# Differential attention: the split of the transposed probabilities moves to ACT and VectorE, the difference of the maps to GpSimd, the scores into one five-bank PSUM tile

## The chip, the cores and the metric

The kernel runs on one core of a Trainium2 chip. The metric is the device time of one execution in microseconds (us). Before the change it was 3203.99 us, the median of three runs (3201.15 to 3204.88).

## The reference, cut to what matters

The program computes one step of a two-layer backbone on 1024 latent tokens and 128 context tokens, all in fp32: in layer 0 differential attention, in layer 1 windowed attention, after each a SwiGLU feed-forward part, with norms and modulation around them. The change touches only the differential attention of the latent tokens: 8 heads, 1024 queries, 1280 keys (256 cached and 1024 own). Each head has two maps of scores with 64 columns each:

```python
s = jnp.einsum('bqhmd,bkhmd->bhmqk', qi, k).astype(jnp.float32) * scale
p = jax.nn.softmax(s, axis=-1)
a = p[:, :, 0] - lam * p[:, :, 1]
return jnp.einsum('bhqk,bkhe->bqhe', a.astype(v.dtype), v)
```

## The kernel before, in words

Matrix products keep fp32 accuracy by splitting an operand into a rounded half (hi) and a remainder (lo), both of type fp32r, and adding three products.

`diff_attention` works on 32 pairs: each of the 8 heads has four pairs of 128-row query blocks. In a pair, i is the block (0 or 1) and m the map (0 or 1). The steps are methods of `Pair`, one letter each:

- S: six matmuls write the 128x1280 scores of (m, i) into PSUM (line 737). The tile has three banks of 512 columns, and there are two such tiles, taken in turn.
- R: VectorE's maximum over the 1280 scores (line 744). E: ACT's exponential of them into SBUF, with the row sum (line 749).
- c: two small VectorE instructions for the factor of map 1 (lines 755 and 756). C: VectorE adds both maps, `a = e1 * factor + e0` (line 761).
- T: TensorE transposes `a`, four 128x128 blocks (two in the last group, g = 2) into one PSUM bank (line 768).
- V: ACT copies the transposed group to SBUF as `a32` (line 773). P: GpSimd rounds it to hi (line 110, the helper `pool_round`) and subtracts for lo (line 784); in the very last pair VectorE does the subtraction.
- A: three matmuls of one key block with the values (lines 793 to 795), ten A per pair. X, B, Y: copy, transpose back, copy out and store.

The order is written out by hand: `ROUND` is a list of tokens, and a token such as T112 means step T, group (or map) 1, block 1, of the pair two rounds back. So E011 and R111 are work on the second block of the pair before, S000 on the first of the present one. Each engine executes its own instructions strictly in the order of this list; engines run beside one another and wait only for what an instruction needs. One pass of the list is a round, there are 32, and `DRAIN` finishes the last pairs. The W token splits a piece of the output weights in every second round (lines 102 and 103).

PSUM has eight banks. Before, the scores take six, the transposes (tag `t`) one, the accumulator `av` one. The exponentials `e` have four SBUF buffers, `a` two.

Two other places are named by the prediction. `turn_hT` (lines 164 and 165) splits a transposed PSUM tile with ACT and VectorE. `Halves.first` (lines 1395 and 1396) lets ACT and VectorE both copy the same transposed PSUM tile; line 1413 is a copy by ACT of the second tile, which for the last, half-wide pair is the same tile as that of line 1396, in columns 64 to 127 instead of 0 to 63 of each block.

Of the kernel before, what the change touches and what calls it, by code (L numbers as in the profile page):

```python
# [9 lines left out]
F32 = mybir.dt.float32  # L10
F32R = mybir.dt.float32r
BF16 = mybir.dt.bfloat16
AF = mybir.ActivationFunctionType
ALU = mybir.AluOpType
AX = mybir.AxisListType
# [3 lines left out]
P = 128  # L19
# [11 lines left out]
DH = 8  # L31
# [13 lines left out]
def hybrid_step(ctx: ExitStack, tc: tile.TileContext, x_prompt, x_sample, cache_diff_k, cache_diff_v,  # L45
# [5 lines left out]
    act, dve, pool, pe = nc.scalar, nc.vector, nc.gpsimd, nc.tensor  # L51
# [57 lines left out]
    def pool_round(out, in_):  # L109
        pool.tensor_scalar(out=out, in0=in_, scalar1=1.0, scalar2=0.0, op0=ALU.mult, op1=ALU.add)  # L110
# [588 lines left out]
    def diff_kv(sb, h):  # L699
        K = sb.tile([P, 2, (NTB + NCB) * P], F32R, name="K")  # L700
        dma(out=K.bitcast(F32), in_=kT_d[0][2 * h:2 * h + 2].rearrange("m p t -> p m t"))
        V = sb.tile([P, NTB + NCB, 2, P], F32R, name="V")
        dma(out=V.bitcast(F32), in_=v_d[0][:, h].rearrange("(t p) f d -> p t f d", p=P))
        return K, V
# [11 lines left out]
    def diff_attention(op, s1_all, wo_pool, pre, kv0, q0):  # L716
        NKB = NCB + 8
        NK = NKB * P
        with sbuf("da") as sb, psum("dap") as ps:
            class Pair:  # L720


                def __init__(self, h, tbs):
                    self.h, self.tbs, self.last = h, tbs, (h, tbs[0]) == (DH - 1, 6)
                    self.S, self.e, self.a, self.s2, self.nm = {}, {}, {}, {}, {}
                    self.tp, self.a32, self.aT, self.kb = {}, {}, {}, 0

                def s1(self, i):
                    return s1_all[:, self.tbs[i], self.h:self.h + 1]

                def step_S(self, m, i):

                    S = self.S[i, m] = ps.tile([P, 3 * 512], F32, name="S", tag="S", bufs=2)
                    for j in range(0, NK, 512):
                        n = min(NK - j, 512)
                        for f in range(2):
                            pe.matmul(S[:, j:j + n], lhsT=self.q[:, f, m, i * P:(i + 1) * P],  # L737
                                      rhs=kv[self.h][0][:, m, j:j + n], start=(f == 0), stop=(f == 1))

                def step_R(self, m, i):  # L740
                    if m == 0:
                        self.nm[i] = sb.tile([P, 2], F32, name="nm", tag="sm", bufs=8)
                        self.s2[i] = sb.tile([P, 2], F32, name="s2", tag="sm", bufs=8)
                    dve.tensor_reduce(out=self.nm[i][:, m:m + 1], in_=self.S[i, m][:, 0:NK], axis=AX.X, op=ALU.max,  # L744
                                      negate=True)

                def step_E(self, m, i):
                    e = self.e[i, m] = sb.tile([P, NK], F32, name="e", tag="e", bufs=4)
                    act.activation(out=e, in_=self.S[i, m][:, 0:NK], func=AF.Exp, bias=self.nm[i][:, m:m + 1],  # L749
                                   accum_out=self.s1(i) if m == 0 else self.s2[i][:, 0:1])  # L750

                def step_c(self, _, i):
# [5 lines left out]
                def step_C(self, _, i):  # L758

                    self.a[i] = sb.tile([P, NK], F32, name="a", tag="a", bufs=2)  # L760
                    dve.scalar_tensor_tensor(out=self.a[i], in0=self.e[i, 1], scalar=self.s2[i][:, 1:2], in1=self.e[i, 0],
                                             op0=ALU.mult, op1=ALU.add)

                def step_T(self, g, i):

                    tp = self.tp[i, g] = ps.tile([P, 4, P], F32, name="tpa", tag="t", bufs=1)
                    for t in range(4 * g, min(4 * g + 4, NKB)):
                        pe.transpose(tp[:, t - 4 * g, :], self.a[i][:, t * P:(t + 1) * P], ident)

                def step_V(self, g, i):  # L770
                    n = min(4, NKB - 4 * g)
                    x = self.a32[i, g] = sb.tile([P, 4, P], F32, name="a32", tag="a32", bufs=2)
                    act.copy(out=x[:, 0:n, :], in_=self.tp[i, g][:, 0:n, :])  # L773

                def step_P(self, g, i):

                    n = min(4, NKB - 4 * g)
                    if g not in self.aT:
                        self.aT[g] = sb.tile([P, 2, 4 if g < 2 else 2, 2 * P], F32R, name="aT",
                                             tag="aT" if g < 2 else "aTb", bufs=4 if g < 2 else 2)  # L780
                    hi, lo = [self.aT[g][:, f, 0:n, i * P:(i + 1) * P] for f in range(2)]
                    x = self.a32[i, g][:, 0:n, :]
                    pool_round(hi, x)
                    (dve if self.last else pool).tensor_tensor(out=lo, in0=x, in1=hi.bitcast(F32), op=ALU.subtract)  # L784

                def step_A(self, _, __):

# [13 lines left out]

                def step_B(self, _, __):

                    self.ot = ps.tile([P, 4, P], F32, name="tpo", tag="t", bufs=1)
                    for i in range(2):
                        pe.transpose(self.ot[:, i, :], self.oT[:, i * P:(i + 1) * P], ident)

                def step_Y(self, _, __):
# [2 lines left out]
                    t0 = self.tbs[0] * P  # L811
                    dma(out=o_d[t0:t0 + 2 * P, self.h * P:(self.h + 1) * P].rearrange("(t p) d -> p t d", p=P), in_=ot)

            pairs = [Pair(h, (tb, tb + 1)) for h in range(DH) for tb in range(0, 8, 2)]
            kv = {0: kv0}
            pairs[0].q = q0
# [2 lines left out]
            def wo_piece(i):  # L819
# [5 lines left out]

            ROUND = ("c001 A003 T012 A003 V202 V102 S000 R111 P213 T112 P002 A003 A003 E011 A003 P202 V012 "
                     "C001 P102 E111 T212 R000 V112 W000 S100 P012 R100 T001 X003 A002 V212 c011 E000 A002 "
                     "A002 B003 S010 V001 C011 Y003 T201 R010 A002 P112 E100 A002 T101 S110").split()  # L830


            DRAIN = ("c001 l1 A003 A003 V202 P213 l0 T012 V102 R111 A003 A003 P002 E011 P202 V012 A003 "
# [3 lines left out]
                     "A001 A001 A001 A001 P211 A001 A001 A001 n0 s11 X001 B001 Y001 n1").split()  # L837
            n = len(pairs)

            def run(token, i):  # L840
                j = i - int(token[-1])
                if token[0] in "lsn":
                    op.early({"l": "load", "s": "stat", "n": "scale"}[token[0]], *[int(x) for x in token[1:]])
                elif token[0] == "W":
                    if i % 2 == 0 and i < 32:
                        wo_piece(i // 2)
                elif 0 <= j < n:
                    getattr(pairs[j], "step_" + token[0])(int(token[1]), int(token[2]))

            with tc.manual_schedule(engines=ENGINES):  # L850
                for i in range(n):
                    if i + 1 < n:
                        x = pairs[i + 1]
                        x.q = diff_q((pre, sb)[(i + 1) % 2], x.h, x.tbs)
                    if i % 4 == 2:
                        h = pairs[i].h + 1
                        if h < DH:
                            kv[h] = diff_kv((pre, sb)[h % 2], h)
                    for token in ROUND:
                        run(token, i)  # L860
                for token in DRAIN:
                    run(token, n)
            return wo

    class Prompts:
# [29 lines left out]
        def score(self, h0):  # L895
            q, e = self.q[h0], self.e[h0]
            nm = small8("nm8")
            for half in range(2):
                ms = slice(4 * half, 4 * half + 4)
                S = self.bank("pS")  # L900
                for m in range(4):
                    for f in range(2):
                        pe.matmul(S[:, m, :], lhsT=q[f][:, 4 * half + m, :], rhs=self.K[h0][:, 4 * half + m, :],
                                  start=(f == 0), stop=(f == 1))
# [61 lines left out]
    def swa_kv(sb, g, rooms=None):  # L966
        K = rooms[0] if rooms else sb.tile([P, (NTB + NCB) * P], F32R, name="K")
        dma(out=K.bitcast(F32), in_=kT_d[1][g])
        V = rooms[1] if rooms else sb.tile([P, NTB + NCB, 2, HD], F32R, name="V")
        dma(out=V.bitcast(F32), in_=v_d[1][:, g].rearrange("(t p) f d -> p t f d", p=P))  # L970
        return K, V
# [10 lines left out]
    def swa_attention(op, wo_pool, pre, kv0, q0):  # L982
        with sbuf("sa") as sb, psum("sap") as ps:
# [133 lines left out]
            for g in range(SKV):  # L1117
                for tbs in ((0, 1), (2, 3), (4, 5), (6, 7)):
                    pair = {"tbs": tbs}
                    for half, tb in enumerate(tbs):  # L1120
# [5 lines left out]

            ROUND = ("S00 R00 T42 E31 C42 K11 A02 A12 E00 T01 S10 L32 L42 C01 K21 L01 "
                     "R10 B03 A22 D03 M03 E10 S20 R20 T11 C11 E20 A32 S30 R30 L11 T21 "
# [5 lines left out]
            with tc.manual_schedule(engines=ENGINES):  # L1134
                for i in range(n + LAST):
# [5 lines left out]
                    if u0 and u0.tb == 4 and u0.g + 1 < SKV:  # L1141
                        kv[u0.g + 1] = swa_kv((pre, sb)[(u0.g + 1) % 2], u0.g + 1)
                    for token in ROUND:
                        j = i - int(token[2])
# [768 lines left out]
    f = la.f  # L1913
# [87 lines left out]
```

## Time and profile before

| | |
|---|---|
| median of 3 runs | 3203.99 us |
| the profiled execution's own time | 3199.07 us |
| its span | 3197.3 us |
| TensorE busy | 3001.8 us (94%) |
| VectorE busy | 2048.6 us (64%) |
| ACT busy | 1421.9 us (44%) |
| GpSimd busy | 1361.9 us (43%) |
| mean granted TensorE clock | 0.981 |

The profile comes from one execution. The span runs from the first to the last instruction. PE is TensorE's matmul, PEld its weight load (which overlaps matmuls), DVE is VectorE, ACT is ScalarE, POOL is GpSimd. Busy shares are means over the whole program; the stage of the change is only some 13% of it, so the rows below are mostly of that stage alone. A granted clock of 1.00 is 2.4 GHz, 0.50 is 1.2 GHz.

### The profile page before, as it was taken

The numbers are of one execution on the slowest core, as the hardware profiler recorded it, in microseconds if no ns is written. First come the engines' busy times: TensorE is split into PE (matmuls) and PEld (weight loads), VectorE is DVE, ScalarE is ACT, GpSimd is POOL, SyncE is SP. The second block draws the span as 40 slices with busy tenths as digits, with TensorE's granted clock in tenths as the row PEclk, the third lists the DMA queues.
The fourth block names the chain that finished last, engine by engine and source line by source line (L and its number), as shares of the span: only waits on it lengthen the run. The fifth ranks groups of instructions, "written<-read, shape, count | busy, mean of one in ns | idle before, by whom it ended". The sixth has DMA issues, their size and how long they took to land.

```text
span 3197.3 us, 47914 instructions
## 1 busy us (share of the span) xinstructions
PE 3001.8 (94%) x17998; PEld 2636.8 (82%) x17998; DVE 2048.6 (64%) x2789; ACT 1421.9 (44%) x2764; POOL 1361.9 (43%) x1186
## 2 busy tenths in 40 slices
PE   8999988998896999999999899999987999999999
PEld 5888777777776999999878787777767999998887
DVE  6786388888566777753786643999567633334544
ACT  6332267777554333333444323777433333333442
POOL 2553289999343444442021343666333433340101
PEclk9999999999998999999999999999988999999999
DMA  6675633332422434335765354433432322226564
GB/s 214 200 228 179 201 112 114 116 118 94 130 100 80 129 109 129 109 97 177 252 216 195 130 173 125 116 115 99 142 107 81 108 64 83 66 80 211 185 199 149
DMA packets 373808, 442.23 MB, mean 138 GB/s; under 512 B 26804, under 2 KB 295644, under 8 KB 373576
## 3 DMA queue, kind: packets, MB, share of 16 engines
q1 hardware_dynamic: 373576, 439.16, 43.6%
q8 instruction: 142, 2.33, 0.3%
q14 instruction: 90, 0.74, 0.1%
HBM read 335.71 MB, written 103.37 MB: 137 GB/s over the span
## 4 chain that ended last, share of the span: by engine, by line
PE 67%; POOL 14%; DVE 9%; ACT 4%; issue 3%; DMA 2%; SPq 1%; DVEq 0%; ACTq 0%; POOLq 0%
POOL aT L784 7%; PE guX L1518 6%; PE guX L1519 6%; PE guX L1520 6%; PE dacc L1635 5%; PE dacc L1637 5%; PE dacc L1636 5%; POOL aT L110 4%; PE qacc L556 4%; PE qacc L558 4%; PE qacc L557 4%; PE guY L1518 3%; PE guY L1520 3%; PE guY L1519 3%; PE guZ L1518 1%
## 5 line engine op out<-in xcount | busy, mean ns | idle before, releaser
L1551 POOL TENSOR_TENSOR sg<-sg,U 128x256 f32<-128x256 f32 x88 | 74.9, 851 | 563.4 <-ACT sg L1550 553.1
L1635 PE MATMUL dacc<-fh,ahl 128*128 128x512 f32 x792 | 312.0, 394 | 2.3 <-DVE U L1554 2.3
L1636 PE MATMUL dacc<-fl,ahl 128*128 128x512 f32 x792 | 310.7, 392 | 0.0
L1637 PE MATMUL dacc<-fh,ahl 128*128 128x512 f32 x792 | 310.7, 392 | 0.0
L556 PE MATMUL qacc<-whi,hh 128*128 128x512 f32 x648 | 259.7, 401 | 1.3 <-ACT hh L431 1.3
L558 PE MATMUL qacc<-whi,hl 128*128 128x512 f32 x648 | 254.9, 393 | 0.0
L557 PE MATMUL qacc<-wlo,hh 128*128 128x512 f32 x648 | 254.2, 392 | 0.6 <-DVE wlo L106 0.6
L154 POOL TENSOR_TENSOR xt<-yacc,xt 128x1024 f32<-128x1024 f32 (+1 forms) x19 | 49.7, 2621 | 459.9 <-DVE yacc L153 242.0
L784 POOL TENSOR_TENSOR aT<-a,aT 128x512 fp32r<-128x512 f32 x186 | 237.3, 1276 | 15.5
L1620 DVE TENSOR_TENSOR fl<-fraw,fh 128x1024 fp32r<-128x1024 f32 x132 | 165.4, 1253 | 121.3 <-ACT fh L1619 120.7
L744 DVE TENSOR_REDUCE nm<-S 128x1 f32<-128x1280 f32 x128 | 190.2, 1486 | 51.1 <-PE S L737 51.1
L1619 ACT CAST fh<-fraw 128x1024 fp32r<-128x1024 f32 x132 | 138.4, 1048 | 170.8 <-DMA fraw<-in_w_down_dram 156.7
L737 PE MATMUL S<-K,q 128*128 128x512 f32 (+1 forms) x768 | 184.5, 377 | 12.9 <-ACT e L749 8.9
L266 DVE SCALAR_TENSOR_TENSOR macc<-wmod,sc,macc 128x512 f32<-128x512 f32 x196 | 186.1, 992 | 0.0
L1635 PEld LDWEIGHTS dacc<-fh,ahl 128*128 128x128 f32 x792 | 149.2, 188 | 36.4 <-DVE U L1554 3.1
L1637 PEld LDWEIGHTS dacc<-fh,ahl 128*128 128x128 f32 x792 | 149.0, 188 | 33.7
L1636 PEld LDWEIGHTS dacc<-fl,ahl 128*128 128x128 f32 x792 | 149.1, 188 | 32.9
L749 ACT ACTIVATE e<-S,nm 128x1280 f32<-128x1280 f32 x128 | 171.4, 1339 | 7.2 <-DVE nm L744 7.1
L737 PEld LDWEIGHTS S<-K,q 128*128 128x128 f32 x768 | 137.5, 193 | 43.8 <-ACT e L749 19.0
L578 ACT CAST xT<-tpx 128x512 fp32r<-128x512 f32 x127 | 68.5, 592 | 236.5 <-issue 125.3
L110 POOL TENSOR_SCALAR aT<-a 128x512 fp32r<-128x512 f32 x192 | 154.0, 802 | 22.7 <-ACT a L773 22.7
L1490 DVE TENSOR_TENSOR fl<-fsum,fh 128x1024 fp32r<-128x1024 f32 x84 | 102.3, 1218 | 81.3 <-ACT fh L1488 81.3
(369 smaller groups left out, 9726.7 us busy)
## 6 DMA issues: line engine op xcount, KB each, us to landing
fraw<-in_w_down_dram SPq DMA_DIRECT2D x132, 512.0 KB
wmod<-in_w_mod_dram SPq DMA_DIRECT2D x112, 256.0 KB
araw<-a_d SPq DMA_DIRECT2D x132, 192.0 KB
fraw<-in_w_gate_dram SPq DMA_DIRECT2D x44, 512.0 KB
fraw<-in_w_up_dram SPq DMA_DIRECT2D x42, 512.0 KB
qT_d<-xT SPq DMA_DIRECT2D x36, 512.0 KB
q<-qT_d SPq DMA_DIRECT2D x64, 256.0 KB
wraw<-in_w_qkv_diff_dram SPq DMA_DIRECT2D x24, 512.0 KB
```

The lines of the kernel that those rows point to most:

```text
L110: pool.tensor_scalar(out=out, in0=in_, scalar1=1.0, scalar2=0.0, op0=ALU.mult, op1=ALU.add)
L556: pe.matmul(acc, lhsT=xh, rhs=hi[:, a, :], start=(kb == 0), stop=False)
L557: pe.matmul(acc, lhsT=xh, rhs=lo[:, a, :], start=False, stop=False)
L558: pe.matmul(acc, lhsT=xl, rhs=hi[:, a, :], start=False, stop=(kb == KB - 1))
L737: pe.matmul(S[:, j:j + n], lhsT=self.q[:, f, m, i * P:(i + 1) * P], rhs=kv[self.h][0][:, m, j:j + n], start=(f == 0), stop=(f == 1))
L784: (dve if self.last else pool).tensor_tensor(out=lo, in0=x, in1=hi.bitcast(F32), op=ALU.subtract)
L1518: pe.matmul(o, lhsT=hi[:, kb, :], rhs=xh[:, kb, :], start=(first and kb == 0), stop=False, **more)
L1519: pe.matmul(o, lhsT=hi[:, kb, :], rhs=xl[:, kb, :], start=False, stop=False, **more)
L1520: pe.matmul(o, lhsT=lo[:, kb, :], rhs=xh[:, kb, :], start=False, stop=(kb == 3), **more)
L1635: pe.matmul(acc, lhsT=ah, rhs=hi[:, cs], start=(d == 0), stop=False)
L1636: pe.matmul(acc, lhsT=ah, rhs=lo[:, cs], start=False, stop=False)
L1637: pe.matmul(acc, lhsT=al, rhs=hi[:, cs], start=False, stop=(d == NDF - 1))
```

## The change

The scores become one tile, allocated once, of five banks (2560 columns): map 0 in columns 0 to 1279, map 1 in columns 1280 to 2559, for every block and pair. Each map's matmuls are cut where a bank ends, three pieces and six matmuls as before (1280 to 1535, 1536 to 2047, 2048 to 2559 for map 1). The bank that this frees gives the transposes a second buffer. V now writes hi (`aT`, fp32r) directly from PSUM, P is a VectorE subtraction that reads PSUM, and `a32` is gone. C becomes two GpSimd instructions. The special case of the last pair goes. ROUND and DRAIN get another order.

```diff
-                    S = self.S[i, m] = ps.tile([P, 3 * 512], F32, name="S", tag="S", bufs=2)
-                    for j in range(0, NK, 512):
-                        n = min(NK - j, 512)
+                    j0 = m * NK
+                    S = self.S[i, m] = scores[:, j0:j0 + NK]
+                    cuts = [0] + [c - j0 for c in range(512, 5 * 512, 512) if j0 < c < j0 + NK] + [NK]
+                    for j, j1 in zip(cuts, cuts[1:]):
                         for f in range(2):
-                            pe.matmul(S[:, j:j + n], lhsT=self.q[:, f, m, i * P:(i + 1) * P],
-                                      rhs=kv[self.h][0][:, m, j:j + n], start=(f == 0), stop=(f == 1))
+                            pe.matmul(S[:, j:j1], lhsT=self.q[:, f, m, i * P:(i + 1) * P],
+                                      rhs=kv[self.h][0][:, m, j:j1], start=(f == 0), stop=(f == 1))
...
-                    dve.tensor_reduce(out=self.nm[i][:, m:m + 1], in_=self.S[i, m][:, 0:NK], axis=AX.X, op=ALU.max,
-                                      negate=True)
+                    dve.tensor_reduce(out=self.nm[i][:, m:m + 1], in_=self.S[i, m], axis=AX.X, op=ALU.max, negate=True)
...
-                    act.activation(out=e, in_=self.S[i, m][:, 0:NK], func=AF.Exp, bias=self.nm[i][:, m:m + 1],
+                    act.activation(out=e, in_=self.S[i, m], func=AF.Exp, bias=self.nm[i][:, m:m + 1],
...
-                    dve.scalar_tensor_tensor(out=self.a[i], in0=self.e[i, 1], scalar=self.s2[i][:, 1:2], in1=self.e[i, 0],
-                                             op0=ALU.mult, op1=ALU.add)
+                    pool.tensor_scalar(out=self.a[i], in0=self.e[i, 1], scalar1=self.s2[i][:, 1:2], scalar2=None,
+                                       op0=ALU.mult)
+                    pool.tensor_tensor(out=self.a[i], in0=self.a[i], in1=self.e[i, 0], op=ALU.add)
...
-                    tp = self.tp[i, g] = ps.tile([P, 4, P], F32, name="tpa", tag="t", bufs=1)
+                    tp = self.tp[i, g] = ps.tile([P, 4, P], F32, name="tpa", tag="t", bufs=2)
...
-                    x = self.a32[i, g] = sb.tile([P, 4, P], F32, name="a32", tag="a32", bufs=2)
-                    act.copy(out=x[:, 0:n, :], in_=self.tp[i, g][:, 0:n, :])
...
-                    pool_round(hi, x)
-                    (dve if self.last else pool).tensor_tensor(out=lo, in0=x, in1=hi.bitcast(F32), op=ALU.subtract)
+                def step_V(self, g, i):
+
+                    x, hi, _ = self.halves(g, i)
+                    act.copy(out=hi, in_=x)
+
+                def step_P(self, g, i):
+
+                    x, hi, lo = self.halves(g, i)
+                    dve.tensor_tensor(out=lo, in0=x, in1=hi.bitcast(F32), op=ALU.subtract)
...
+            scores = ps.tile([P, 5 * 512], F32, name="S", tag="S", bufs=1)
...
-            ROUND = ("c001 A003 T012 A003 V202 V102 S000 R111 P213 T112 P002 A003 A003 E011 A003 P202 V012 "
-                     "C001 P102 E111 T212 R000 V112 W000 S100 P012 R100 T001 X003 A002 V212 c011 E000 A002 "
-                     "A002 B003 S010 V001 C011 Y003 T201 R010 A002 P112 E100 A002 T101 S110").split()
+            ROUND = ("c001 A003 T012 A003 V102 E011 S000 R111 P102 T112 A003 V012 A003 P012 C001 A003 T212 "
+                     "V112 E111 R000 P112 W000 S100 T001 V212 R100 P212 X003 A002 c011 E000 A002 A002 B003 "
+                     "V001 S010 C011 P001 Y003 T201 A002 R010 V201 E100 A002 T101 P201 S110").split()
```

The helper `halves` returns the transposed group in PSUM and the two halves of `aT` that it is split into.

## Rows read from the trace of the kernel before

**Rows 1.** Busy time by engine in one stretch of the stage (busy us, instruction count).

```profile
core 0: us, PE busy (x) PEld busy (x) DVE busy (x) ACT busy (x) POOL busy (x), PEclk, DMA share, GB/s
600.00:700.00 100.00, 89.88 (x596) 78.28 (x594) 87.16 (x84) 71.07 (x130) 96.00 (x96) 1.00 0.38 121
```

**Rows 2.** The chain of waits, 370 to 860 us; pieces are start, duration, what.

```profile
by line: POOL aT L784 47.6%; POOL aT L110 29.2%; issue 4.0%; ACT junk L1265 2.0%; PE S L737 1.7%; SPq L888 1.6%; DMA V<-o_d 1.5%; PE qacc L558 1.1%; PE qacc L556 1.1%; PE qacc L557 1.1%; DVE nm L744 0.9%; DMA wraw<-in_w_o_diff_dram 0.9%; SP
...
463.76 1.84 POOL aT L110
...
783.63 1.83 POOL aT L110
```

**Rows 3.** Lines 110 and 784 over the whole trace: ns minimum/median/maximum, forms.

```profile
L110 POOL TENSOR_SCALAR aT<-a x192: 404/617/1873, 406.0 to 811.7; 128x512 fp32r<-128x512 f32 x128, 128x256 fp32r<-128x256 f32 x64
...
L784 POOL TENSOR_TENSOR aT<-a,aT x186: 725/1287/2393, 406.7 to 803.0; 128x512 fp32r<-128x512 f32 x124, 128x256 fp32r<-128x256 f32 x62
```

**Rows 4.** Instruction groups by shape, 450 to 700 us: total busy us, mean ns.

```profile
L744 DVE TENSOR_REDUCE nm<-S 128x1 f32<-128x1280 f32 x79 | 117.4, 1486 | 30.9 <-PE S L737 30.9
...
L761 DVE SCALAR_TENSOR_TENSOR a<-e,s 128x1280 f32<-128x1280 f32 x40 | 79.8, 1996 | 0.7
...
L773 ACT COPY a<-tpa 128x512 f32<-128x512 f32 x79 | 46.4, 587 | 37.1 <-POOL aT L784 32.3 <-PE tpa L768 4.8
...
L756 DVE SCALAR_TENSOR_TENSOR s<-s_all,neglam,s 128x1 f32<-128x1 f32 x39 | 14.2, 363 | 1.4
...
L755 DVE RECIPROCAL s<-s 128x1 f32<-128x1 f32 x39 | 5.9, 152 | 0.0
```

**Rows 5.** Line 165, a VectorE subtraction that reads PSUM, over the trace.

```profile
L165 DVE TENSOR_TENSOR hl<-tp_n,hh x30: 673/680/693, 57.9 to 1831.2; 128x512 fp32r<-128x512 f32 x30
```

**Rows 6.** Instructions in order of time: start, us, what, [idle before, releaser].

```profile
906.24 0.59 ACT L1395 CAST B11h<-tp_n 128x512 fp32r<-128x512 f32 x1 [0.25 <-PE tp_n L1388]
...
906.85 1.29 DVE L1396 COPY raw<-tp_n 128x512 f32<-128x512 f32 x2 [0.47 <-ACT B11h L1395]
...
2420.52 0.74 DVE L1396 COPY raw<-tp_n 128x256 f32<-128x256 f32 x2
...
2421.29 0.37 ACT L1413 COPY raw<-tp_n 128x256 f32<-128x256 f32 x1 [3.65 <-DVE raw L1396]
```

**Rows 7.** In order of time, a round's TensorE work: scores, transposes, values.

```profile
604.65 0.46 PEld L768 LDWEIGHTS tpa<-ident,a 128*128 128x128 f32 x4
604.75 0.60 PE L768 MATMUL tpa<-ident,a 128*128 128x128 f32 x4
...
605.54 0.28 PE L793 MATMUL av<-aT,V 128*128 128x256 f32 x1
...
605.90 0.28 PE L793 MATMUL av<-aT,V 128*128 128x256 f32 x1
...
610.63 1.23 PEld L737 LDWEIGHTS S<-K,q 128*128 128x128 f32 x6
610.66 1.41 PE L737 MATMUL S<-K,q 128*128 128x512 f32 x6
```

**Rows 8.** The chain of waits where the stage starts, one behind the other.

```profile
394.32 2.52 PE S L737 x6
396.86 1.50 DVE nm L744
398.39 1.43 ACT e L749 x2
399.86 4.54 PE S L737 x12
```

**Rows 9.** TensorE's granted clock: two stretches, and an instruction behind an idle time.

```profile
394.32:396.84 2.52, 2.52 (x7) 2.10 (x8) 0.75 (x1) 1.42 (x2) 0.00 (x0) 0.50 0.95 367
...
992.04 1.31 PE L1388 MATMUL tp_n<-ident,xn 128*128 128x128 f32 x8 [2.42 <-DVE raw L1396]
...
992.00:996.00 4.00, 3.93 (x32) 3.73 (x33) 3.43 (x6) 2.48 (x5) 0.00 (x0) 1.00 0.04 12
```

More of the change, by code (lines that the diff above doesn't have):

```diff
@@ L723, in __init__ @@
                 def __init__(self, h, tbs):
-                    self.h, self.tbs, self.last = h, tbs, (h, tbs[0]) == (DH - 1, 6)
+                    self.h, self.tbs = h, tbs
                     self.S, self.e, self.a, self.s2, self.nm = {}, {}, {}, {}, {}
-                    self.tp, self.a32, self.aT, self.kb = {}, {}, {}, 0
+                    self.tp, self.aT, self.kb = {}, {}, 0
                 def s1(self, i):
@@ L760, in step_C, with halves @@
                     self.a[i] = sb.tile([P, NK], F32, name="a", tag="a", bufs=2)
-                    dve.scalar_tensor_tensor(out=self.a[i], in0=self.e[i, 1], scalar=self.s2[i][:, 1:2], in1=self.e[i, 0],
-                                             op0=ALU.mult, op1=ALU.add)
+                    pool.tensor_scalar(out=self.a[i], in0=self.e[i, 1], scalar1=self.s2[i][:, 1:2], scalar2=None,
+                                       op0=ALU.mult)
+                    pool.tensor_tensor(out=self.a[i], in0=self.a[i], in1=self.e[i, 0], op=ALU.add)
                 def step_T(self, g, i):
-                    tp = self.tp[i, g] = ps.tile([P, 4, P], F32, name="tpa", tag="t", bufs=1)
+                    tp = self.tp[i, g] = ps.tile([P, 4, P], F32, name="tpa", tag="t", bufs=2)
                     for t in range(4 * g, min(4 * g + 4, NKB)):
                         pe.transpose(tp[:, t - 4 * g, :], self.a[i][:, t * P:(t + 1) * P], ident)
-                def step_V(self, g, i):
-                    n = min(4, NKB - 4 * g)
-                    x = self.a32[i, g] = sb.tile([P, 4, P], F32, name="a32", tag="a32", bufs=2)
-                    act.copy(out=x[:, 0:n, :], in_=self.tp[i, g][:, 0:n, :])
-                def step_P(self, g, i):
+                def halves(self, g, i):
                     n = min(4, NKB - 4 * g)
@@ L780, in step_P @@
                                              tag="aT" if g < 2 else "aTb", bufs=4 if g < 2 else 2)
-                    hi, lo = [self.aT[g][:, f, 0:n, i * P:(i + 1) * P] for f in range(2)]
-                    x = self.a32[i, g][:, 0:n, :]
-                    pool_round(hi, x)
-                    (dve if self.last else pool).tensor_tensor(out=lo, in0=x, in1=hi.bitcast(F32), op=ALU.subtract)
+                    return self.tp[i, g][:, 0:n, :], *[self.aT[g][:, f, 0:n, i * P:(i + 1) * P] for f in range(2)]
+                def step_V(self, g, i):
[4 more added lines that the diff above has]
+                    dve.tensor_tensor(out=lo, in0=x, in1=hi.bitcast(F32), op=ALU.subtract)
                 def step_A(self, _, __):
@@ L802, in step_B @@
                 def step_B(self, _, __):
-                    self.ot = ps.tile([P, 4, P], F32, name="tpo", tag="t", bufs=1)
+                    self.ot = ps.tile([P, 4, P], F32, name="tpo", tag="t", bufs=2)
                     for i in range(2):
@@ L823, in wo_piece @@
                 wsplit(raw, wo[kb][0][:, cs], wo[kb][1][:, cs])
-            ROUND = ("c001 A003 T012 A003 V202 V102 S000 R111 P213 T112 P002 A003 A003 E011 A003 P202 V012 "
-                     "C001 P102 E111 T212 R000 V112 W000 S100 P012 R100 T001 X003 A002 V212 c011 E000 A002 "
-                     "A002 B003 S010 V001 C011 Y003 T201 R010 A002 P112 E100 A002 T101 S110").split()
-            DRAIN = ("c001 l1 A003 A003 V202 P213 l0 T012 V102 R111 A003 A003 P002 E011 P202 V012 A003 "
[3 rows of a table removed]
-                     "A001 A001 A001 A001 P211 A001 A001 A001 n0 s11 X001 B001 Y001 n1").split()
+            ROUND = ("c001 A003 T012 A003 V102 E011 S000 R111 P102 T112 A003 V012 A003 P012 C001 A003 T212 "
+                     "V112 E111 R000 P112 W000 S100 T001 V212 R100 P212 X003 A002 c011 E000 A002 A002 B003 "
+                     "V001 S010 C011 P001 Y003 T201 A002 R010 V201 E100 A002 T101 P201 S110").split()
+            DRAIN = ("c001 l1 A003 A003 T012 l0 V102 R111 P102 A003 T112 A003 V012 E011 P012 A003 C001 "
[3 rows of a table added]
+                     "A001 A001 A001 A001 n0 s11 X001 B001 Y001 n1").split()
             n = len(pairs)
```

6 rows, old and new, of the table DRAIN are left out of this document.

## The prediction, made before the changed kernel was run

> **What bounds the kernel now.** Of the 3197.3 us span the change touches one stage, differential attention over the latent blocks, roughly from 387 to 815 us. I read the stretch table first [rows 1]: in 100 us of that stage GpSimd is busy 96%, TensorE 90, VectorE 87, ACT 71. Busy shares alone do not name the bound, so the chain of waits comes next [rows 2]: from 370 to 860 us, 77% of it is GpSimd, the two split instructions of line 784 and line 110, one behind the other without a hole. The same step comes back at 463.76 and, 25 rounds later, at 783.63 us: 319.87 / 25 = 12.79 us per round, one pair of query blocks per round. GpSimd's 96% of that is 12.3 us.
>
> Why so much: of its line 110 the 512-wide median is 617 ns, but the maximum is 1873 [rows 3]; the chain's 1.84 us pieces are such ones.
>
> **The change part by part.**
>
> *The split leaves GpSimd.* Six line-110 and six line-784 instructions per pair go; ACT's copy writes the rounded half directly, at the price it has now (587 ns per 512-wide copy [rows 4]); VectorE subtracts out of PSUM. The nearest row is line 165, the same operation with the same operands at 673 to 693 ns [rows 5]. Four at 0.68 and two half-wide ones at about 0.4 (my estimate from that row) make 3.5 us on VectorE.
>
> *The difference moves to GpSimd.* VectorE loses two of line 761, 2 x 2.0 us [rows 4]. GpSimd gets a multiplication by a per-partition scalar and an addition, both 1280 wide. Line 110 costs 404 ns at 256 columns and 617 at 512, so 0.617 + 3 x 0.213 = 1.26 us; line 784 costs 725 and 1287, so 1.287 + 3 x 0.562 = 2.97 [rows 3]. Together 4.25 us with the gap. The scalar from memory on GpSimd has no row; at worst it costs what a two-operand instruction costs, which makes 5.95 us; at best line 110's floor twice, 2.5. I take 4.25: both forms have rows at two widths.
>
> *Engine loads after.* VectorE: maxima 4 x 1.49, the small c steps 2 x (0.15 + 0.36) [rows 4], 3.5 for the subtractions, about 0.4 for output-weight pieces: 10.9 us. GpSimd 8.5, ACT as before 9.1 (71% of 12.79), TensorE no more than its 90%, 11.5. By loads alone a round could fall from 12.79 to about 11.5.
>
> *Scores in five banks.* Two tiles of three banks become one tile of 2560 columns. Map 0 has columns 0 to 1279, map 1 has 1280 to 2559, a bank is 512 columns: both maps lie in the third bank. The maximum (R) and the exponential (E) each read a whole map in one instruction, so each of them reads that bank. The question is whether two accesses to different columns of one bank may overlap. The trace has an answer [rows 6]. At 906.83 ACT ends a copy out of a transposed tile, and at 906.85 VectorE starts reading the same tile, after 0.47 us idle that ACT ended. VectorE's copy takes nothing from ACT's; both only read. At 2420.52 VectorE reads columns 0 to 63 of each block of such a tile (two copies, until 2421.26), and ACT's copy of columns 64 to 127 starts at 2421.29 after 3.65 us idle ended by VectorE. Other bytes, no data passed, only the bank in common: a read waits for a read. So I take it that every S, R and E of both maps runs alone on the third bank, in the order of the tokens: E011 S000 R111 E111 R000 S100 R100 E000 S010 R010 E100 S110. The one relief is that a map-1 S writes the third bank first.
>
> A rule speaks against this layout too. The Trainium skill, page "PSUM — Partial Sum Buffer", section Terms, says that two engines on the same bank and quadrant at once are an error, reads against reads included. By it the round is the serial sum below; without it the accesses are free and the round is that of the byte rival. [Rows 6] agree with the page.
>
> *The sum of a round.* Per step: S writes for 1.41 us and issues for 1.23 [rows 7]; R 1.49 [rows 4]; E with its accumulator read 1.43, hand-offs 0.02 to 0.04 [rows 8]. Start the clock at S000.
> - S000 ends 1.41. R111 (which ran free before) waits for it: 1.45 to 2.94.
> - E111 cannot follow at once. Ahead of it in ACT's queue stands V112, which needs T112, whose PSUM tile P102 must free, and P102 is queued behind R111 on VectorE: P102 to 3.62, T112 (0.60 [rows 7]) to 4.26, V112 (0.59) to 4.88, E111 to 6.31. Cost of this: 1.9 us.
> - R000 (second read of the bank, behind E111) to 7.83, S100 to 9.28, R100 to 10.80, E000 to 12.26, S010 to 13.71, R010 to 15.23, E100 to 16.69.
> - S110 issues from 16.73 for 1.23; behind it on TensorE stand A003, T012, A003 (0.36, 0.46, 0.36 [rows 7]) before S000 comes round. V102 and E011 on ACT end at about 18.7 and are hidden behind these. Next S000 at 19.14.
>
> The round is 19.14 us instead of 12.79, 6.35 more. Beside it everything else is hidden: GpSimd's C011 starts at about 11.8, ends at 16.1 and is wanted by E011 at 17.3 and T012 at 18.3, so even 5.95 us a piece would cost 0.1 us a round; the stretched instructions of [rows 3] go, which is worth nothing on this path, and so is the second bank for the transposes, whose waits on ACT's copies lie off this path. Over the 31 steps from first to last S000: 197 us. Round 0 has no pair before it and lacks R111 to E111, 4.9 us. At the end the last difference takes 4.25 instead of 2.0 and the last splits are about 1.2 shorter: 1 more. In all +193.
>
> The profiled execution took 3199.07 us with a span of 3197.3, 1.8 around it. 3199 + 193 = 3392; the median of the runs shown, 3203.99, lies 4.9 above this execution, so the forecast against it is 3397 us. If V112's wait goes (another order in the queues), 1.9 us per round less: 3338; if each hand-off costs 0.1 more, 12 x 0.1 x 31 = 37 more: 3434.
>
> **The rivals.**
>
> *The clock falls as well* (chance 0.11). TensorE would stand still some 2.2 us before T112 and again before S100. At the granted clock of 0.50, that is 1.2 GHz, S took 2.52 us instead of 1.41 [rows 8, 9]. If it fell in every round: three S by 1.1, T112 by 0.5, the queue from S110 by 2.4, 6.2 us x 31 = +192, 3590; in one round of three 3460. Against it: after an idle 2.42 us at 992.04 the granted clock stayed 1.00, that is 2.4 GHz [rows 9].
>
> *Only writes order the bank, reads do not exclude each other* (0.09). R000 then runs beside E111 and E000 beside R100. S000 to E111 6.31 as before, S100 to 7.76, R100 to 9.28, P212 0.4, c011 0.55, C011 on GpSimd 4.25 to 14.5, E011 (its e buffer is the one C011 reads) to 16.0. 3.2 x 31 = +99: 3303. Against it [rows 6], which are reads alone.
>
> *Order by bytes, and the difference on GpSimd becomes the loop* (0.06). No shared-bank waits: S000, T112 behind its issue to 1.84, V112 2.46, E111 3.90, S100 5.35, R100 6.85, P212 and c011 7.8, C011 12.1, E011 13.5, S000: 13.55 per round, +24: 3228.
>
> *Faster* (0.04). The same byte order, but GpSimd's C is not late. The loop above shrinks with C: it equals 12.79 at C = 3.5 us and leaves TensorE's 11.5 as the bound at about 2.2. Place: the e buffer between C011 and E011. Gain (12.79 - 11.5) x 31 = 40: 3164. For it: GpSimd is the bound today and the loads fall. Against it: both rows of C, and [rows 6].
>
> **How the numbers follow.** The serial bank has 0.70, and its own range is 3335 to 3435. For 8 in 10 I add the lighter end of the clock rival above and the write-only rival below: 3290 to 3460. A difference under 0.2% (6.4 us) cannot be told from none. Faster: the last rival, 0.04. Slower: 0.94, the four other cases (0.96) less 0.02 for a byte loop that comes out shorter than worked out; that 0.02 is the chance of within 0.2%.
>
> **What would show it.** In the profile after, VectorE's maxima should stand idle until ACT's exponential ends, ACT's exponential until a maximum of the other map, and S until a maximum rather than an exponential; the same step returns every 19 us; in the chain of waits GpSimd has almost no share and S, R and E share it; GpSimd is busy some 45%, TensorE near 60. The subtraction out of PSUM stands at 0.68 us, GpSimd's pair at 1.26 and 2.97. Wrong if R000 starts while E111 runs, if the round is below 16 us, or if S shows 2.5 us in many rounds.

## The result and the profile after

The changed kernel takes 3455.23 us (median of six runs, 3451.08 to 3457.66) against 3201.61 of the kernel before in the same sessions: ratio 1.0789, 95% interval 1.0775 to 1.0803. The forecast was 3397 us, range 3290 to 3460. The span grew from 3197.3 to 3449.1 us, by 251.8 us.

The stretch table first, as in [rows 1]: busy us of each engine in 100 us, with the count of instructions, then the granted clock.

```profile
core 0: us, PE busy (x) PEld busy (x) DVE busy (x) ACT busy (x) POOL busy (x), PEclk, DMA share, GB/s
600.00:700.00 100.00, 65.64 (x373) 55.14 (x372) 53.73 (x72) 44.94 (x82) 62.45 (x20) 0.93 0.27 85
400.00:500.00 100.00, 63.40 (x282) 51.61 (x282) 45.07 (x60) 39.28 (x69) 57.79 (x18) 0.73 0.17 53
```

No engine is near its limit any more: GpSimd falls from 96 to 62, TensorE from 90 to 66, VectorE from 87 to 54. When every engine idles, something makes them take turns. The chain of waits, in which GpSimd was to have almost no share, cannot say what: in this profile it begins at 1142.09 us, behind the stage. Who waited for whom in the stage can be read, 500 to 900 us (total us, times, longest):

```profile
PE S L738 <- ACT e L749: 57.4, 59, 1.8
...
PE S L738 <- DVE nm L745: 25.7, 20, 1.4
```

In a round S waits three times for an E and once for a maximum, and no engine's wait in that list of 17 ends with GpSimd. Why they wait shows in order of time. One round, from one T112 (700.64) to the next (721.16); start, duration, engine and line, what, and in brackets the idle time before it and what ended it:

```profile
700.64 1.09 PE L769 MATMUL tpa<-ident,a 128*128 128x128 f32 x4 [2.34 <-DVE aT L786]
...
702.25 1.34 ACT L749 ACTIVATE e<-S,nm 128x1280 f32<-128x1280 f32 x1
...
703.71 1.49 DVE L745 TENSOR_REDUCE nm<-S 128x1 f32<-128x1280 f32 x1 [2.61 <-ACT e L749]
...
705.26 1.43 PE L738 MATMUL S<-K,q 128*128 128x256 f32 x6 [1.29 <-DVE nm L745]
...
706.73 1.49 DVE L745 TENSOR_REDUCE nm<-S 128x1 f32<-128x1280 f32 x1 [0.92 <-PE S L738]
...
708.31 1.33 ACT L749 ACTIVATE e<-S,nm 128x1280 f32<-128x1280 f32 x1 [3.66 <-DVE nm L745]
709.07 3.52 POOL L761 TENSOR_SCALAR a<-e,s 128x1280 f32<-128x1280 f32 x1 [7.29 <-DVE s L756]
...
709.78 1.43 PE L738 MATMUL S<-K,q 128*128 128x512 f32 x6 [0.68 <-ACT e L749]
...
711.32 1.49 DVE L745 TENSOR_REDUCE nm<-S 128x1 f32<-128x1280 f32 x1 [0.39 <-PE S L738]
...
712.67 2.91 POOL L763 TENSOR_TENSOR a<-a,e 128x1280 f32<-128x1280 f32 x1
...
712.90 1.33 ACT L749 ACTIVATE e<-S,nm 128x1280 f32<-128x1280 f32 x1 [1.06 <-DVE nm L745]
...
714.37 1.43 PE L738 MATMUL S<-K,q 128*128 128x256 f32 x6 [1.79 <-ACT e L749]
...
715.89 1.33 ACT L749 ACTIVATE e<-S,nm 128x1280 f32<-128x1280 f32 x1 [1.10 <-PE S L738]
...
717.37 1.45 PE L738 MATMUL S<-K,q 128*128 128x512 f32 x6 [0.41 <-ACT e L749]
...
718.92 1.49 DVE L745 TENSOR_REDUCE nm<-S 128x1 f32<-128x1280 f32 x1 [3.32 <-PE S L738]
...
721.16 1.09 PE L769 MATMUL tpa<-ident,a 128*128 128x128 f32 x4 [2.34 <-DVE aT L786]
```

Read the E, R and S lines alone, top to bottom: E111, R000, S100, R100, E000, S010, R010, E100, S110, E011, S000, R111. Each starts within 0.15 us of the end of the one before, although six of the eleven hand-offs join different maps, which have no data in common (E111 to R000, R000 to S100, R100 to E000, R010 to E100, S110 to E011, S000 to R111). The twelfth, R111 to E111, holds the queue of P102, T112 and V112. That is the serial chain, in the order forecast.

The groups by shape, 500 to 900 us (total busy us, mean ns of one, then idle time before them):

```profile
L761 POOL TENSOR_SCALAR a<-e,s 128x1280 f32<-128x1280 f32 x39 | 137.4, 3524 | 149.5 <-DVE s L756 147.5 <-PE S L738 2.0
L745 DVE TENSOR_REDUCE nm<-S 128x1 f32<-128x1280 f32 x79 | 117.8, 1492 | 135.5 <-PE S L738 83.3 <-ACT e L749 52.2
L763 POOL TENSOR_TENSOR a<-a,e 128x1280 f32<-128x1280 f32 x39 | 113.1, 2900 | 3.3
L749 ACT ACTIVATE e<-S,nm 128x1280 f32<-128x1280 f32 x78 | 103.7, 1330 | 114.5 <-DVE nm L745 93.6 <-PE S L738 21.0
...
L786 DVE TENSOR_TENSOR aT<-tpa,aT 128x512 fp32r<-128x512 f32 x78 | 51.7, 684 | 27.3 <-ACT aT L781 27.3
...
L786 DVE TENSOR_TENSOR aT<-tpa,aT 128x256 fp32r<-128x256 f32 x40 | 16.6, 415 | 0.0
```

R (line 745) costs what it did [rows 4], but stood idle 52.2 us until an E had ended. The subtraction out of PSUM is 684 ns, as [rows 5] gave it. GpSimd's multiplication takes 3524 ns where 1260 was expected, its addition 2900 where 2970 was.

The last table is the clock in the same round: around T112 and during S100.

```profile
700.60:701.40 0.80, 0.76 (x5) 0.79 (x5) 0.50 (x1) 0.00 (x0) 0.80 (x1) 0.50 0.00 0
701.40:703.50 2.10, 2.10 (x12) 2.10 (x11) 0.00 (x0) 1.73 (x3) 0.38 (x1) 0.50 0.00 0
705.20:706.60 1.40, 1.34 (x7) 1.13 (x8) 0.60 (x2) 0.00 (x0) 0.00 (x0) 1.00 0.00 0
```

After 2.34 us of idling TensorE is granted 0.50 (1.2 GHz) for some 3 us, then 1.00 again. T112 takes 1.09 us instead of 0.60 [rows 7].

### The profile page after: what moved, and what is told of

It reads as the page before. It is cut to its first block, busy times and chain, and to the rows that moved or that the text cites. A ratio compares the mean times of both kernels' runs of the same rounds, so it can differ in the third digit from the quotient of the medians.

```text
span 3449.1 us, 47933 instructions
## 1 busy us (share of the span) xinstructions
PE 3067.0 (89%) x17998; PEld 2683.9 (78%) x17998; DVE 2040.5 (59%) x2911; ACT 1421.7 (41%) x2764; POOL 1387.2 (40%) x936
## 4 chain that ended last, share of the span: by engine, by line
PE 52%; DVE 8%; ACT 3%; issue 2%; POOL 2%; DMA 1%; DVEq 0%; SPq 0%; ACTq 0%; POOLq 0%
PE guX L1524 5%; PE guX L1522 5%; PE guX L1523 5%; PE dacc L1639 5%; PE dacc L1640 5%; PE dacc L1641 5%; PE guY L1522 3%; PE guY L1524 3%; PE guY L1523 3%; PE guZ L1522 1%; PE guZ L1524 1%; PE guZ L1523 1%; PE qacc L556 1%; PE qacc L557 1%; PE qacc L558 1%
## 5 line engine op out<-in xcount | busy, mean ns | idle before, releaser
L761 POOL TENSOR_SCALAR a<-e,s 128x1280 f32<-128x1280 f32 x64 | 225.5, 3524 | 252.9 <-DVE s L756 249.3
L738 PE MATMUL S<-K,q 128*128 128x512 f32 (+1 forms) x768 | 192.8, 389 | 148.7 <-ACT e L749 100.7
L763 POOL TENSOR_TENSOR a<-a,e 128x1280 f32<-128x1280 f32 x64 | 185.6, 2899 | 5.3
L769 PE MATMUL tpa<-ident,a 128*128 128x128 f32 x640 | 121.1, 312 | 74.4 <-DVE aT L786 71.5
L781 ACT CAST aT<-tpa 128x512 fp32r<-128x512 f32 x192 | 98.1, 512 | 179.5 <-PE tpa L769 179.5
```

The costliest lines, as they stand in the source:

```text
L738: pe.matmul(S[:, j:j1], lhsT=self.q[:, f, m, i * P:(i + 1) * P], rhs=kv[self.h][0][:, m, j:j1], start=(f == 0), stop=(f == 1))
L761: pool.tensor_scalar(out=self.a[i], in0=self.e[i, 1], scalar1=self.s2[i][:, 1:2], scalar2=None, op0=ALU.mult)
```

## The experiments

The theory on record was that the shared third **bank** puts S, R and E in a row. Ten kernels tell it from its rivals: the **tile** does it (one allocation, wherever its pieces lie), GpSimd's difference does it, or the clock.

**1. P102 ahead of S000 and R111** takes away the queue that held T112 back. Edit to the changed kernel:

```diff
-            ... V102 E011 S000 R111 P102 T112 ...
+            ... V102 E011 P102 S000 R111 T112 ...
```

> The changed kernel with one token moved: P102 ahead of S000 and R111, so that VectorE frees the transposes' bank before it goes into the maximum that waits for the shared bank. Theory (accesses to the third bank run one after another, and the queue P102 - T112 - V112 adds a wait inside that chain): E111 follows R111 at once, some 2.3 us of the measured 20.5 us round go, round about 18.2, time about 3455 - 2.3 x 31 = 3384 us (3370 to 3400). Rival (GpSimd's difference, now 6.4 us a piece, or the clock sets the round): the round stays, 3440 us or more.

Measured: 3407.16 us, ratio 1.0642 [1.0626, 1.0657] (the brackets are the 95% interval), 48 us less than the change and 7 above the range expected. E111 now follows R111 at once, but the scores of map 1 and some transposes run at half clock for part of their time:

```profile
700.90 1.33 ACT L749 ACTIVATE e<-S,nm 128x1280 f32<-128x1280 f32 x1 [0.63 <-DVE nm L745]
...
703.89 2.27 PE L738 MATMUL S<-K,q 128*128 128x256 f32 x6 [1.94 <-DVE nm L745]
```

S100 takes 2.27 us (granted clock 0.56 from 703.90 to 706.20) and S110 2.03, where the change had 1.43 for both. So the queue is real, and part of what its removal gives the clock takes back.

**2. Each map in banks of its own, still one tile.** On top of 1: one six-bank tile, map 1 from column 1536 on; this leaves the transposes one bank.

```diff
-                    j0 = m * NK
+                    j0 = m * 1536
-            scores = ps.tile([P, 5 * 512], F32, name="S", tag="S", bufs=1)
+            scores = ps.tile([P, 6 * 512], F32, name="S", tag="S", bufs=1)
-                    ... name="tpa", tag="t", bufs=2)
+                    ... name="tpa", tag="t", bufs=1)
```

> The kernel with P102 moved, and the two maps in three banks each (columns 0 to 1279 and 1536 to 2815), which leaves one bank for the transposes. Nothing else differs. Theory (the shared bank is the cause): R, E and S of the two maps run beside one another again; what is left is GpSimd's loop through the e buffer: S000 issue 1.24, T112 0.60, V112 0.59, E111 1.43, S100 1.41, R100 1.49, P212 0.41, c 0.55, C011 6.42, E011 1.43, hand-offs 0.3: about 15.9 us per round, time about 3201 + 3.1 x 31 = 3297 us (3270 to 3320). Rival (the sharing costs nothing and the queue order or GpSimd does it all): the same as the kernel with P102 moved, 3384, or more, because a bank for the transposes is lost.

Measured: 3563.79 us, ratio 1.1131 [1.1115, 1.1148], where 3297 was expected. The theory of the bank falls: no bank is shared, and the row stays.

```profile
702.66 1.33 ACT L749 ACTIVATE e<-S,nm 128x1280 f32<-128x1280 f32 x1
...
704.11 1.49 DVE L745 TENSOR_REDUCE nm<-S 128x1 f32<-128x1280 f32 x1 [3.21 <-ACT e L749]
```

R000 reads banks 0 to 2, E111 reads banks 3 to 5, and R000 still waits 3.21 us until E111 has ended.

**3. The same two maps in two tiles.** Only the allocation differs from 2: the same six banks, the same order, the same single transpose bank.

```diff
-            scores = ps.tile([P, 6 * 512], F32, name="S", tag="S", bufs=1)
+            scores = [ps.tile([P, 3 * 512], F32, name="S", tag=f"S{m}", bufs=1) for m in range(2)]
```

> As the kernel with three banks per map in one tile, but the maps are two PSUM tiles of three banks. Banks, columns, instructions and token order are the same; only the allocation differs. Theory (accesses by different engines to one PSUM tile are put one behind another, whatever their banks): the waits of R000 for E111 and of R111 for S000 go, GpSimd's loop of 15.9 us is left: about 3297 us (3270 to 3330). Rival (the order of the tokens or the single bank for the transposes makes the 24.3 us round): 3540 us or more.

Measured: 3338.76 us, ratio 1.0426 [1.0411, 1.0442], 225 us less than 2. R now starts while an E of the other map runs. These are E011, R111, R000 and E111:

```profile
699.44 1.33 ACT L748 ACTIVATE e<-S,nm 128x1280 f32<-128x1280 f32 x1
...
700.19 1.48 DVE L744 TENSOR_REDUCE nm<-S 128x1 f32<-128x1280 f32 x1
...
702.60 1.49 DVE L744 TENSOR_REDUCE nm<-S 128x1 f32<-128x1280 f32 x1 [0.21 <-PE S L737]
...
703.62 1.33 ACT L748 ACTIVATE e<-S,nm 128x1280 f32<-128x1280 f32 x1
```

R111 runs beside E011, and R000, which in 2 waited for E111, starts ahead of it, as soon as its own S000 has ended. That is the decisive pair. It stays 42 us above what I expected of it. Its waits, 500 to 700 us (total, times, longest):

```profile
ACT aT L780 <- PE tpa L768: 73.0, 63, 2.2
...
PE tpa L768 <- DVE s L754: 24.5, 12, 2.1
...
PE tpa L768 <- DVE aT L785: 19.6, 24, 1.1
```

Largest is ACT waiting for a transpose, and the transposes wait for VectorE: with one bank, each needs the subtraction out of it done, which stands in VectorE's queue behind maxima. With the tiles parted the rest of the change thus still costs 136 us against the kernel before; how much of that is the single transpose bank, the order or GpSimd's difference was not parted.

**4. One transpose bank, shared score bank kept.** Kernel 1 with the transposes' `bufs=2` made 1. It parts the two things in which 2 differed from 1.

> The order of p102_first (P102 ahead of S000 R111), the five shared score banks kept, but one bank for the transposes in place of two, as own_banks has it. It parts the two things in which own_banks differed from p102_first (3407): where map 1 lies inside the one score tile, and the second transpose bank. Theory 1 (the waits go by the score tile, and the bank in which a piece lies is without weight): the lost transpose bank is all that own_banks paid for, so this comes to own_banks' time, 3564 (3540 to 3590), with its round of 24.3 us. Theory 2 (the distant columns of own_banks did something of their own, good or bad): it stands off from 3564 by over 30; if keeping the maps in banks of their own was worth something within one tile, this is slower, 3600 to 3750; if the second transpose bank is nearly free, it stays at 3407 to 3440.

Measured: 3562.2 us, ratio 1.1126 [1.1108, 1.1145], the time of 2 to within 2 us.

```profile
698.86 1.33 ACT L749 ACTIVATE e<-S,nm 128x1280 f32<-128x1280 f32 x1
...
700.31 1.49 DVE L745 TENSOR_REDUCE nm<-S 128x1 f32<-128x1280 f32 x1 [3.21 <-ACT e L749]
```

The wait of R000 is the same 3.21 us as in 2. In one tile it makes no difference whether the maps share a bank; the second transpose bank, which I had called worth nothing, is worth 155 us in that order (3562.2 - 3407.2).

**5. One tile alone, in the kernel before.** Nothing of the change but a single tile for all scores; E011 moves ahead of S000, since with one tile the old order would hold S000 behind a later E.

```diff
-                    S = self.S[i, m] = ps.tile([P, 3 * 512], F32, name="S", tag="S", bufs=2)
+                    S = self.S[i, m] = scores[:, m * 1536:m * 1536 + 1536]
+            scores = ps.tile([P, 6 * 512], F32, name="S", tag="S", bufs=1)
-            ROUND = "... V202 V102 S000 R111 P213 T112 P002 A003 A003 E011 A003 ..."
+            ROUND = "... V202 V102 E011 S000 R111 P213 T112 P002 A003 A003 A003 ..."
```

> The kernel before, with one part of the change alone: the scores are one tile, allocated once, here of six banks, so no bank is shared; E011 stands ahead of S000, which that needs. Theory (one tile, one access at a time): S, R and E of both maps run in series, 4 x (1.43 + 1.41 + 1.49) + 12 hand-offs of 0.05 = 17.9 us per round instead of 12.79, time about 3201 + 5.1 x 31 = 3359 us, up to 3400 if the clock falls. Rival (only a shared bank costs, or the split and GpSimd's difference do): 3201 within 10 us.

Measured: 3462.06 us, ratio 1.0813 [1.0797, 1.0829], above the range expected. This part, with E011's new place, costs as much as the whole change, with the split still on GpSimd; the new place was not run alone. R000, at 703.89 us, again starts only as E111 ends (703.85). The waits, 500 to 700 us, and S100 at half clock:

```profile
ACT e L749 <- DVE nm L744: 88.8, 29, 4.2
DVE nm L744 <- PE S L737: 83.8, 29, 6.1
```

```profile
705.44 2.50 PE L737 MATMUL S<-K,q 128*128 128x512 f32 x6 [0.59 <-DVE nm L744]
```

In this round S100, S010 and the S110 behind them take 2.50, 2.48 and 2.24 us instead of 1.41, together 3.0 us more. The time lies 103 us above the 3359 expected, 3.3 a round: in this round the clock makes up most of it.

**6. The difference back on VectorE.** The changed kernel with C as one `scalar_tensor_tensor` again. E011 starts in the changed kernel 0.31 us after GpSimd's difference ends (715.58) and 0.09 after S110's last matmul (715.80); this tells which one it waits for.

> The changed kernel with the difference of the maps back on VectorE, one instruction as before; five banks kept. Theory (the serial bank sets the round, GpSimd's difference is beside it): nothing but E011 can gain. If E011 waits for GpSimd to release its e buffer, it starts 0.6 to 1.0 us earlier and the round falls by about 0.6: 3437 us; if it waits for the last matmul of S110, the time stays at 3455 within 10 us. Rival (moving the difference to GpSimd is the main loss): 3300 us or less.

Measured: 3448.98 us, ratio 1.0774 [1.0756, 1.0792], not to be told from the change (1.0775 to 1.0803).

```profile
708.70 1.55 DVE L761 SCALAR_TENSOR_TENSOR a<-e,s 128x1280 f32<-128x1280 f32 x1
...
714.11 1.43 PE L738 MATMUL S<-K,q 128*128 128x256 f32 x6 [1.73 <-ACT e L749]
...
715.63 1.33 ACT L749 ACTIVATE e<-S,nm 128x1280 f32<-128x1280 f32 x1 [1.10 <-PE S L738]
```

The difference is done at 710.25, and E011 still starts 0.09 us after S110's last matmul. GpSimd's difference lies beside the path.

**7. A constant in GpSimd's multiplication.** Kernel 2 with -0.25 as an immediate in place of the factor that is read from memory, plus 0 (so the factor of map 1 is left out).

```diff
-  pool.tensor_scalar(out=self.a[i], in0=self.e[i, 1], scalar1=self.s2[i][:, 1:2], scalar2=None, op0=ALU.mult)
+  pool.tensor_scalar(out=self.a[i], in0=self.e[i, 1], scalar1=-0.25, scalar2=0.0, op0=ALU.mult, op1=ALU.add)
```

> As the kernel with three banks per map, but the multiplication on GpSimd takes a constant instead of the factor per row (so the factor of map 1 is left out). It measures what the factor read from memory costs. Theory (the factor from memory makes the instruction 3.5 us instead of the 1.26 worked out from the constant form): the instruction takes about 1.3 us, the loop through GpSimd shortens by 2.2 us a round, time about 3297 - 68 = 3229 us. Rival (the 1280 columns or sharing with VectorE make it slow): the instruction stays near 3.5 us and the time at 3297.

Measured: 3558.26 us, ratio 1.1112 [1.1095, 1.1128], the time of 2 within the intervals; both expected times, 3229 and 3297, stood on the theory that 2 refuted.

```profile
L761 POOL TENSOR_SCALAR a<-e 128x1280 f32<-128x1280 f32 x33 | 41.8, 1266 | 254.3 <-PE tpa L768 140.1 <-ACT e L749 114.1
```

1266 ns: the 1.26 worked out from [rows 3] holds for a constant. With the factor from memory the same width takes 3521 in kernel 2 (3524 in the change).

**8. and 9. The part of the idea that relieves GpSimd, with the two score tiles kept.** In the kernel before, ACT makes the hi half of some groups by a second copy straight from PSUM; GpSimd keeps only the subtraction there. In 8 for group 0, in 9 for groups 0 and 2.

```diff
                 def step_V(self, g, i):
...
                     act.copy(out=x[:, 0:n, :], in_=self.tp[i, g][:, 0:n, :])
+                    if g in (0,):
+                        act.copy(out=self.halves(g, i)[0], in_=self.tp[i, g][:, 0:n, :])
...
                 def step_P(self, g, i):
...
-                    pool_round(hi, x)
+                    if g not in (0,):
+                        pool_round(hi, x)
```

> The kernel before, where ACT writes the rounded half of the first transposed group (g = 0) straight from PSUM by a second copy, and GpSimd only subtracts there. GpSimd loses two 512-wide line-110 instructions per round (0.62 to 1.87 us each), ACT gains two copies of 0.59 and goes from 9.1 to 10.3 us. Theory (before, GpSimd's 12.3 us set the round): the round falls to about 11.5, TensorE's share, 3201 - 1.2 x 31 = 3164 us (3155 to 3180). Rival (the one transpose bank, held 0.6 us longer, sets it): 3195 us or more.

> The kernel before, in which ACT makes the fp32r halves of groups 0 and 2 straight from PSUM with a second copy, and GpSimd only subtracts there (act_rounds_g0 did it for group 0 alone: 3172.8, round 11.98 us, PE 95, VectorE 93, ACT 85, GpSimd 81 of 100). Per round GpSimd loses 2 x 0.415 = 0.83 us more, ACT gains 2 x about 0.36 = 0.7 us (85 to 91 of 100). Theory 1 (after group 0 TensorE and VectorE bound the round, GpSimd no longer): nothing more to win, 3172 (3160 to 3185). Theory 2 (GpSimd's subtraction still sets when the products can start): 3150 or below. Theory 3 (ACT becomes the bound: its copy of group 2 delays E): 3190 to 3215.

Measured: 8 takes 3172.76 us, ratio 0.9907 [0.989, 0.9923], 0.9% faster than the kernel before, a small gain, but its interval leaves out 1; 9 takes 3179.15 us, ratio 0.9931 [0.9916, 0.9945]. The stretch table of 8, then of 9:

```profile
600.00:700.00 100.00, 95.44 (x646) 84.64 (x645) 92.68 (x91) 84.82 (x158) 80.94 (x86) 1.00 0.41 131
```

```profile
600.00:700.00 100.00, 93.39 (x630) 82.72 (x629) 87.30 (x88) 86.73 (x170) 76.98 (x67) 1.00 0.39 123
```

In 8 GpSimd falls from 96 [rows 1] to 81, while TensorE is at 95 and VectorE at 93, and the clock stays at 1.00. Taking still more from GpSimd, in 9, gains nothing. Both times lie in the ranges expected of them.

**10. The split as the change makes it, for group 2 alone**, in the kernel before, with its two score tiles and its one transpose bank: ACT writes hi from PSUM, VectorE subtracts out of PSUM, and P of group 2 moves up beside its V.

```diff
+                    if g == 2:
+                        act.copy(out=self.halves(g, i)[0], in_=self.tp[i, g][:, 0:n, :])
+                        return
...
+                    if g == 2:
+                        dve.tensor_tensor(out=lo, in0=self.tp[i, g][:, 0:n, :], in1=hi.bitcast(F32), op=ALU.subtract)
+                        return
```

> The kernel before, where the half-wide group (g = 2) is split as in the change: ACT rounds from PSUM, VectorE subtracts from PSUM. GpSimd loses about 2.5 us per round, VectorE gains 0.84 and comes to about 12.0. Theory (GpSimd set the round before): 12.0 to 12.3 us, 3201 - 0.6 x 31 = 3182 us (3170 to 3190). Rival (VectorE's queue then delays the release of the transpose bank): 3200 us or more.

Measured: 3268.94 us, ratio 1.0209 [1.0194, 1.0224]: slower, although GpSimd falls to 60. Its waits, 500 to 700 us:

```profile
PE tpa L768 <- DVE s L755: 26.4, 13, 2.1
...
PE tpa L768 <- DVE aT L790: 17.6, 14, 1.3
```

Here the release of the one transpose bank hangs on VectorE's subtraction (line 790), with a 1.5 us maximum ahead of it in the queue, as in 3. Where line 755 is named, that subtraction ended 0.07 us before it: 602.18 against 602.25, and the transposes start at 602.32.

## Why the prediction was right, and where it was not

**Direction, place and form held.** Rounds from 483.55 to 1037.07 us (the same GpSimd instruction, 27 rounds apart) are 553.52 / 27 = 20.50 us each; 19.14 was forecast and 12.79 was before [rows 2]. 31 x (20.50 - 12.79) = 239 of the 251.8 us. Loads fell on every engine, and the time rose, because S, R and E went one by one in the order written down. The time came out 58 us above the forecast. The round at 700 us by its pieces, from start to start (after: from the round shown, whose own S000 starts at 696.88):

| piece of the round | forecast | after |
|---|---|---|
| S000 to R000 | 6.34 | 6.83 |
| R000 to S110 | 10.39 | 10.66 |
| S110 to the next S000 | 2.41 | 3.00 |

**The step that failed: "the one relief is that a map-1 S writes the third bank first", with V102 and E011 hidden.** E011 does not start once the third bank is written; it starts 0.09 us after S110's last matmul, and S000 waits for E011 in turn: 1.43 + 0.09 + 1.48 = 3.00 us instead of 2.41. That fits a rule by tile, with which E011 waits as long as S110 writes any part of it. Experiment 6 shows that nothing of GpSimd's is in it.

**The reason behind it was wrong in name.** [Rows 6] are two engines on one tile, and that tile is one bank: they could not tell a rule on banks from one on tiles. Experiments 2 and 4 agree to within 2 us with and without a shared bank; 3 splits the tile and takes 225 us off; 5 brings the loss into the kernel before with one tile and no shared bank. So the unit of the wait is the tile. In the changed kernel the third bank and the tile are shared by the same steps, so both rules give the same order but for that one relief: that the forecast held with the wrong one was luck. A tile is a name that the program gives to a piece of PSUM, and 2 and 3 issue the same instructions on six banks; that speaks for a wait that the program's allocation brings with it and not the banks, but where it is put in was not looked at. The Trainium skill, page "PSUM — Partial Sum Buffer", section Terms, states its rule for two engines on the same bank and quadrant. In 2 R000 waits 3.21 us for E111 with no bank in common, so that rule does not account for the wait. Whether two engines on one bank would also hold each other up is not shown: in every kernel with a shared bank the tile is shared as well, and a layout with two tiles in one bank was not tried.

**Mis-sized: the clock.** It was given 0.11 as a rival that decides; it came in part. T112 at 1.09 us instead of 0.60 makes 0.49 us, as much as the first line of the table is over. The stage also starts at 0.50 (400.00 to 416.50 us): the two rounds from 416.51 us, at 0.57 and 0.77, take 24.54 and 22.01 us, 5.5 us more than two later ones. Of the 251.8 us about 7 are not traced to a place.

**Mis-sized, without weight: C on GpSimd.** 3.52 + 2.90 = 6.42 us, outside the bounds of 2.5 to 5.95; the factor from memory makes the difference (experiment 7). It is hidden, as said, and by experiment 6 worth no more than the noise. GpSimd's share of 62 instead of 45 is this.

**The queue of P102** was put at 1.9 us a round. Removing it gave 48 us or, over 31 steps, 1.5 us. In the round at 700 us of experiment 1, E111 starts 2.25 us sooner behind R111 than after the change; of this the clock takes back 0.84 us at S100 and most of 0.96 from S110 to the next S000.

**Put at nothing: the second transpose bank**, "worth nothing on this path". Its reason was that waits on ACT's copies lie off the path; but after the change VectorE's subtraction releases the bank as well, as its own term for P102 has it. In the order of experiment 1 the second bank is worth 155 us (4); 3 and 10, with one bank, show transposes waiting for VectorE. In the order as submitted a single bank was not run.

**One sign was stated against the prediction's own order.** It has S wait "until a maximum rather than an exponential"; in the order that it lists, three of the four S of a round stand behind an E, and the profile has 57.4 us of S waiting for an E and 25.7 for a maximum.

## What to carry to other kernels

Merging two PSUM tiles into one to save a bank can cost more than an engine's whole relief: here each S, R and E on the merged tile waited for the one before it in the written order, whatever its engine and columns. When work moves to an engine that releases a buffer, count what stands ahead of the release in that engine's queue, and keep a second buffer. The part of a change that eases the bound can be had alone, as here: a second ACT copy for one group of the three gave 0.9907 of the time before, with the tiles left as they were.

## What the runs showed of the hardware

A GpSimd multiplication by a per-partition factor read from memory took 3524 ns at 1280 columns, by a constant 1266 ns (two operations in the latter; experiments 2 and 7, which differ only in this instruction, have 3521 and 1266).

Where VectorE's two-operand C and GpSimd's subtraction overlap in kernel 8, the one that starts later takes longer in the places shown. C starts at 598.97, and GpSimd's instruction at 599.67 takes 1.99 us instead of 1.28; GpSimd is at work from 604.39 to 606.41, and C at 605.16 takes 2.59 instead of 1.54. GpSimd's first, then VectorE's:

```profile
599.67 1.99 POOL L791 TENSOR_TENSOR aT<-a,aT 128x512 fp32r<-128x512 f32 x1 [0.66 <-ACT aT L782]
...
604.39 2.02 POOL L791 TENSOR_TENSOR aT<-a,aT 128x256 fp32r<-128x256 f32 x2
...
609.71 1.28 POOL L791 TENSOR_TENSOR aT<-a,aT 128x512 fp32r<-128x512 f32 x1
```

```profile
598.97 1.54 DVE L761 SCALAR_TENSOR_TENSOR a<-e,s 128x1280 f32<-128x1280 f32 x1
605.16 2.59 DVE L761 SCALAR_TENSOR_TENSOR a<-e,s 128x1280 f32<-128x1280 f32 x1
```

With GpSimd idle in the stage (experiment 6) C's mean is 1547 ns, against 1996 before [rows 4]. The stretched instructions of [rows 3] fit this; that all of them are such was not tested.

An idle of 2.34 us before T112 went with a granted clock of 0.50, while 2.42 us of it at another place left 1.00 [rows 9], and in kernel 2 the same 2.34 us stood ahead of a T112 of 1.09 us (701.05, granted 0.50) and ahead of one of 0.63 (725.33, granted 1.00). What tells them apart the runs do not show.
